# Feature-major input and output in a two-layer float32 encoder trunk

## The chip, the cores and the metric

The kernel runs on one core of a Trainium2 chip. Its time is the device time of one execution in microseconds (us), median of the runs shown. Engines are named as in the profile: PE (TensorE, matmuls and transposes), PEld (its weight loads, which overlap it), DVE (VectorE), ACT (ScalarE), POOL (GpSimd) and SP (SyncE, which here only issues DMAs). PE's clock has two levels, 1.2 and 2.4 GHz; the profile shows the granted one as a share of 2.4 GHz.

## The reference

Two layers (`DEPTH` = 2) work on x of 512 positions by 1024 features, all in float32. Cut to what matters:

```python
for l in range(DEPTH):
    xn = rms_norm(x, norm1_g[l])
    aq, ak, av, bq, bk, bv, cq, ck, cv, cg, gates = split(xn @ w_in[l])
    ya = dilated_mixer(rope(norm(aq)), rope(norm(ak)), av)     # 6 heads, 3 groups
    yb = diff_attention(rope(norm(bq)), rope(norm(bk)), bv)    # 4 heads, two softmax maps each
    yb = rms_norm(yb, b_out_norm_g[l]) * (1.0 - lam_init)      # per head
    yc = silu(cg) * rms_norm(retention(cq, ck, cv), c_out_norm_g[l])   # 4 heads
    g = sigmoid(gates)
    x = x + (g[0]*(ya @ w_br_a[l]) + g[1]*(yb @ w_br_b[l]) + g[2]*(yc @ w_br_c[l])) @ w_o[l]
    x = x + relu(rms_norm(x, norm2_g[l]) @ w_mlp1[l]) ** 2 @ w_mlp2[l]
```

## The kernel before

**Data.** Inside, x lies feature-major: eight tiles of 128 features by 512 positions. Every float32 product is made of three matmuls on rounded halves: a tensor is split into `hi` (a rounded copy, written by ACT) and `lo` (the rest, by DVE), and `gemm` adds hi·hi, hi·lo and lo·hi. In the tile names an `h` or `l` at the end is such a half (`xgh`, `xgl`: x times the norm's gain; `ynh`, `ynl`: a branch's output; `whi`, `wlo`: weights).

**Stages.** The list `sequence` gives the order of the products of a layer: `A` 0 to 2, `cg`, `C` 0 and 1, `B` 0 to 3 (query, key and value columns of one wave each), the gates `G`, the branch outputs `W`, the output product `O`, and then `M1` and `M2`, the two MLP products, in four rounds. Each works in four PSUM banks (`acc`); `pm` holds four more banks for everything else. `G` 1 0 and `G` 1 1 stand right ahead of `W` 1 0 and `W` 1 1, which multiply branch B's four outputs. Weights come in units of two row tiles by SP (`fetch`, four `raw` buffers) and are split a unit ahead (`refine`, two buffers each). `gemm` runs through the units of a product, all four banks for each, and calls `hooks` at the start of a unit and `done` for each bank of the last.

**Order.** Attention runs beside the products as side threads: `thread_prep` (norm and rotation of q and k), `thread_a`, `thread_b` and `thread_c`. In `build` a planner adds up estimated costs per engine and lets a side thread make a step wherever DVE and ACT lie behind PE by its estimate; a thread yields `("need", flag)` until a flag is set, or `("wait", name)` until PE has gone on for `W[name]` us of the estimate. Before, `thread_prep` needs only that a wave's product is done. A scheduler then orders the instructions of each engine, and each engine keeps that order. The rotated q and k of a wave stand in one of two buffers (`qp`, tag `qk`).

**Branch B.** A head ends in `head_norm`: `ps_b_tail` (weighted values, PSUM) is copied to `y` by ACT, turned by four transposes (`ps_yt`), squared and summed by ACT, brought to 1/sqrt by some ten DVE instructions of four columns (`hf` to `hg`), multiplied (`yn`), turned back by four transposes (`ps_yb`) and split into `ynh` and `ynl`.

**Both ends.** x lies position-major in memory. In `main`, 32 transposes (`ps_main`, L823 on) turn the eight input tiles; DVE copies each to `xt`, POOL writes it to `xspill` for the residual of layer 0, and ACT squares the input with a running sum (`sqx`), so that the first norm needs no transposes. `norm_stat` turns the sum into `nr` (1/sqrt per position); the four `acc` banks of A 0 are emptied with `nr` as scale, so A 1 starts after it. In the last layer `M2` is made position-major, for which `thread_xtok` turns x back (32 transposes, `ps_thread_xtok`, each half's eight copies by ACT and DVE), and `done` scales by `r2` per partition and writes 256 KB blocks. In layer 0, `M2` is feature-major and scaled by `rB2`, the statistic spread over partitions by four transposes (`norm_spread`).

The last layer's block as it was:

```python
self.stt(x, b, self.r2[:, o:o + 1], x, OP.mult, OP.add)
eng = self.nc.sync if o % 2 else self.nc.scalar
eng.dma_start(self.outv[:, o, s[2] * 512:(s[2] + 1) * 512], x)
```

Of the kernel before, what the change touches and what calls it, by code (L numbers as in the profile page):

```python
# [65 lines left out]
def weight_plan(sequence):  # L66
    """The weight blocks in the order of use: (array, layer, first row tile, row tiles, columns per row tile)."""
    units, chunks = [], {}
    r = lambda a, n: list(range(a, a + n))
    for l in range(DEPTH):  # L70
        for s in sequence:
# [19 lines left out]
            first = len(units)  # L91
            for k in range(k0, k1, 2):
                units.append((name, l, (k, cols), min(2, k1 - k), sum(c for _, c in cols)))
# [4 lines left out]
def pack_weights(inputs, sequence):  # L98
    """Every weight block laid out as it lands on chip: row in the tile, row tile, column."""
    out = []  # L100
    for (name, l, (k, cols), n, c) in weight_plan(sequence)[0]:
        w = inputs[name][l, k * P:(k + n) * P]
        w = np.concatenate([w[:, a:a + m] for a, m in cols], axis=1)
        out.append(w.reshape(n, P, c).transpose(1, 0, 2).reshape(-1))
    return np.concatenate(out)


class Trunk:
# [44 lines left out]
    def act(self, out, in_, func=AF.Copy, **k):  # L153
        self.cost["ACT"] += 0.19 + self.size(out) / 1000
        self.nc.scalar.activation(out, in_, func, **k)  # L155
# [19 lines left out]
    def stt(self, out, a, s, b, op0, op1):  # L175
        self._d(out, 1.1)
        self.nc.vector.scalar_tensor_tensor(out, a, s, b, op0=op0, op1=op1)  # L177
# [64 lines left out]
    # ---------------------------------------------------------------- weights  # L242
# [58 lines left out]
    # ---------------------------------------------------------------- set-up  # L301
    def setup(self):
# [3 lines left out]
        self.x4 = []  # L306
        rows = self.U((36, P), name="rows")
        nc.scalar.dma_start(rows, a["rows"])
        nc.sync.dma_start(self.blob[:, 0:P], a["blob"][:, 0:P])
        xv = a["x"][0].rearrange("(p j) d -> p j d", j=NJ)  # L310
# [11 lines left out]
        self.fetch(4)  # L322
# [4 lines left out]
        self.identr = cp.tile([P, P], FR, name="identr")  # L327
        self.act(self.identr, self.ident)
        self.gcol = cp.tile([P, 36], FT, name="gcol")
        pt = self.ps(name="ps_setup")  # L330
        self.tr(pt[:, 0:36], rows, self.ident[0:36, 0:36])
        nc.vector.tensor_copy(self.gcol, pt[:, 0:36])
# [5 lines left out]
        self.xspill = [self.dp.tile([KD, P, SEQ], FT, name=f"xspill{l}") for l in range(DEPTH)]  # L338

    def setup2(self):  # L340
        nc, cp, b = self.nc, self.cp, self.blob
        lam = self.tiny(8, "lam", 1)
# [38 lines left out]
    # ---------------------------------------------------------------- norm of x  # L381
# [3 lines left out]
    def norm_feed(self, k, xt):  # L385
# [3 lines left out]
        if "ss" in st:  # L389
            return  # L390
# [32 lines left out]
    # ---------------------------------------------------------------- prep of q, k, v  # L423
# [42 lines left out]
    def prep(self, w, jp):  # L466
# [37 lines left out]
        self.tt(lo, o8, hi_of(s.bitcast(FT)), OP.subtract)  # L504
        yield ("wait", "prep")
# [13 lines left out]
    # ---------------------------------------------------------------- attention pieces  # L519
# [270 lines left out]
    def thread_prep(self, l):  # L790
        first = True
        for s in self.sequence:
# [3 lines left out]
            if first:  # L796
                self.rope_gains(l)
# [11 lines left out]
    # ---------------------------------------------------------------- main stream  # L809
# [7 lines left out]
    def main(self):  # L817
        nc = self.nc
        self.norm_open(0, 0)
        self.refine(AHEAD + 1)  # L820
        self.nrm["ss"] = self.tiny(16, "ss0", 1)
        for k in range(KD):
            b = self.ps(name="ps_main")  # L823
            for j in range(NJ):
                src = self.x4[(k // 2) * 2 + j // 2][:, j % 2, (k % 2) * P:(k % 2 + 1) * P]
                self.tr(b[:, j * P:(j + 1) * P], src, self.ident)
            self.norm_feed(k, b)
            xt = self.U(name="xt")
            self.copy(xt, b, "DVE")
            nc.gpsimd.dma_start(self.xspill[0][k], xt)  # L830
            for i in range(2):
                scr = self.U((P, 256), name="sqx")
                self.act(scr, self.x4[k][:, i, :], AF.Square,
                         accum_out=self.nrm["ss"][:, 4 * (k // 2) + 2 * (k % 2) + i:4 * (k // 2) + 2 * (k % 2) + i + 1])
            yield
        self.x4 = None
        self.setup2()
        for l in range(DEPTH):
            yield from self.layer(l, self.nrm["xg"])

    def layer(self, l, xg):
# [15 lines left out]
        for s in self.sequence:  # L857
            c = self.ch[l, s]
            kind = s[0]
            if kind in ("A", "B", "C"):  # L860
# [4 lines left out]
                w = self.wave_buffers(kind)  # L865
                self.waves[l, kind, s[1]] = w
# [218 lines left out]
```

## Time and profile before

| | us |
|---|---|
| median of 3 runs | 1811.63 (1811.3 to 1813.87) |
| span of the profiled execution | 1812.9 |
| PE busy in it | 1784.7 (98%) |
| DVE, ACT, POOL busy | 1051.4, 795.4, 186.4 |
| granted TensorE clock, mean | 0.994 of full |

The profile is one execution; its span runs from its first to its last instruction. Its own device time is not among the runs shown, so the span stands for it: it lies 0.07% above the median. A row of a timeline gives the start, the length of the instruction (of `xN` of them from the first to the end of the last), engine, line, operation, what is written `<-` what is read, and in brackets how long the engine was idle before it and what ended that. Matmuls overlap, so what one costs is the distance to the next start, not its length.

### The profile page before, as it was taken

The numbers are of one execution on the slowest core, as the hardware profiler recorded it, in microseconds if no ns is written. First come the engines' busy times: TensorE is split into PE (matmuls) and PEld (weight loads), VectorE is DVE, ScalarE is ACT, GpSimd is POOL, SyncE is SP. The second block draws the span as 40 slices with busy tenths as digits, with TensorE's granted clock in tenths as the row PEclk, the third lists the DMA queues.
The fourth block names the chain that finished last, engine by engine and source line by source line (L and its number), as shares of the span: only waits on it lengthen the run. The fifth ranks groups of instructions, "written<-read, shape, count | busy, mean of one in ns | idle before, by whom it ended". The sixth has DMA issues, their size and how long they took to land.

```text
span 1812.9 us, 22187 instructions
## 1 busy us (share of the span) xinstructions
PE 1784.7 (98%) x8433; PEld 1481.1 (82%) x8433; DVE 1051.4 (58%) x1963; ACT 795.4 (44%) x1469; POOL 186.4 (10%) x177
## 2 busy tenths in 40 slices
PE   7999999999999999999999999999999999999999
PEld 6878978877888888888888888788778878888887
DVE  7676787877465333333576767777865552233433
ACT  5555655645334332322345556455543343333241
POOL 1000000011043111111220000000111321111010
PEclk8999999999999999999999999999999999999999
DMA  6221222222233223223332112222212422323222
GB/s 223 88 70 44 85 70 62 79 70 70 82 119 125 93 93 105 93 93 104 105 105 82 65 44 85 71 64 82 80 63 91 141 80 96 102 93 97 101 94 82
DMA packets 49243, 162.78 MB, mean 90 GB/s; under 512 B 5580, under 2 KB 7792, under 8 KB 49008
## 3 DMA queue, kind: packets, MB, share of 16 engines
q1 hardware_dynamic: 45952, 151.91, 25.7%
q0 software_dynamic: 2560, 8.39, 1.4%
q8 instruction: 66, 1.08, 0.3%
q10 hardware_dynamic: 624, 1.07, 0.2%
q14 instruction: 41, 0.34, 0.1%
HBM read 155.05 MB, written 6.29 MB: 89 GB/s over the span
## 4 chain that ended last, share of the span: by engine, by line
PE 93%; DVE 4%; issue 1%; ACT 1%; POOL 0%; DMA 0%; SPq 0%; ACTq 0%; POOLq 0%; DVEq 0%
PE acc L218 81%; PE ps_c_head L218 2%; PE ps_b_scores L218 1%; PE ps_prep L222 1%; PE ps_a_tail L218 1%; PE ps_to_keys L222 1%; PE ps_b_tail L218 1%; PE ps_a_diag_scores L218 1%; PE ps_a_dense_scores L218 1%; DVE wlo L166 1%; DVE xgl L177 1%; DVE part L166 0%; DVE xr L166 0%; PE ps_yt L222 0%; PE ps_yb L222 0%
## 5 line engine op out<-in xcount | busy, mean ns | idle before, releaser
L166 DVE TENSOR_TENSOR wlo<-raw,whi 128x1024 fp32r<-128x1024 f32 (+2 forms) x296 | 351.4, 1187 | 485.9 <-ACT whi L155 484.1
L155 ACT ACTIVATE whi<-raw 128x1024 fp32r<-128x1024 f32 (+2 forms) x296 | 300.0, 1014 | 632.2 <-PE acc L218 558.2
L218 PE MATMUL acc<-xgh,whi 128*128 128x512 f32 x960 | 380.5, 396 | 0.0
L218 PE MATMUL acc<-xgl,whi 128*128 128x512 f32 x960 | 375.7, 391 | 0.0
L218 PE MATMUL acc<-xgh,wlo 128*128 128x512 f32 x960 | 374.8, 390 | 0.0
L218 PEld LDWEIGHTS acc<-xgh,whi 128*128 128x128 f32 x960 | 180.6, 188 | 39.5 <-issue 3.1
L218 PEld LDWEIGHTS acc<-xgh,wlo 128*128 128x128 f32 x960 | 180.6, 188 | 38.3
L218 PE MATMUL acc<-whi,xgh 128*128 128x384 f32 (+1 forms) x576 | 208.7, 363 | 1.5 <-DVE vl L177 0.8
L218 PEld LDWEIGHTS acc<-xgl,whi 128*128 128x128 f32 x960 | 180.8, 188 | 35.4
L218 PE MATMUL acc<-wlo,xgh 128*128 128x384 f32 (+1 forms) x576 | 202.8, 352 | 2.0 <-DVE wlo L166 2.0
L218 PE MATMUL acc<-whi,xgl 128*128 128x384 f32 (+1 forms) x576 | 201.0, 352 | 0.1
L163 POOL TENSOR_TENSOR gate<-gate,gate 128x512 f32<-128x512 f32 x32 | 50.4, 1590 | 926.5 <-DVE gate L177 562.8
L163 POOL TENSOR_TENSOR rl<-rl 128x512 f32<-128x512 f32 x64 | 78.5, 1236 | 537.4 <-ACT hh L155 429.7
L218 PEld LDWEIGHTS acc<-whi,xgh 128*128 128x128 f32 x576 | 109.6, 191 | 13.2 <-issue 5.4
L218 PEld LDWEIGHTS acc<-wlo,xgh 128*128 128x128 f32 x576 | 109.9, 191 | 7.6 <-DVE wlo L166 2.3
L218 PEld LDWEIGHTS acc<-whi,xgl 128*128 128x128 f32 x576 | 109.5, 190 | 6.5 <-issue 0.7
L218 PE MATMUL acc<-hh,wlo 128*128 128x512 f32 x256 | 99.7, 389 | 0.9 <-DVE wlo L166 0.9
L218 PE MATMUL acc<-hl,whi 128*128 128x512 f32 x256 | 99.6, 389 | 0.0
L218 PE MATMUL acc<-hh,whi 128*128 128x512 f32 x256 | 99.6, 389 | 0.0
L218 PE MATMUL acc<-whi,hh 128*128 128x512 f32 x256 | 99.6, 389 | 0.0
L218 PE MATMUL acc<-wlo,hh 128*128 128x512 f32 x256 | 99.6, 389 | 0.0
L218 PE MATMUL acc<-whi,hl 128*128 128x512 f32 x256 | 99.6, 389 | 0.0
(218 smaller groups left out, 2741.8 us busy)
## 6 DMA issues: line engine op xcount, KB each, us to landing
raw<-in_weights_dram SPq DMA_DIRECT2D x236, 512.0 KB, 3.3
raw<-in_weights_dram SPq DMA_DIRECT2D x56, 384.0 KB, 3.1
xr<-xspill POOLq DMA_DIRECT2D x16, 256.0 KB, 4.1
x<-in_x_dram SPq DMA_DIRECT2D x8, 256.0 KB, 5.8
xspill<-xt POOLq DMA_DIRECT2D x8, 256.0 KB, 3.5
xspill<-xr POOLq DMA_DIRECT2D x8, 256.0 KB, 2.3
blob<-in_blob_dram SPq DMA_DIRECT2D x1, 1024.0 KB
raw<-in_weights_dram SPq DMA_DIRECT2D x4, 256.0 KB, 2.6
```

What stands on the lines that cost most here:

```text
L155: self.nc.scalar.activation(out, in_, func, **k)
L163: self.nc.gpsimd.tensor_tensor(out, a, b, op=op)
L166: self.nc.vector.tensor_tensor(out, a, b, op=op)
L177: self.nc.vector.scalar_tensor_tensor(out, a, s, b, op0=op0, op1=op1)
L218: self.nc.tensor.matmul(out, lhsT, rhs, start=start, stop=stop)
L222: self.nc.tensor.transpose(out, in_, ident)
```

## The change

x enters as an array of eight feature-major tiles and is loaded straight into the tiles `xt`, in turn with the first weight units, of which the first two have one row tile instead of two; identity and gains come over ACT's queue, the gains already turned (`cols` for `rows`). The transposes, the copies and the writes to `xspill` at the start are gone; layer 0's residual reads the input. The first norm is made as the others are: `norm_square` (ACT squares a tile, POOL adds it to the sum), then four transposes of the sum (`ps_norm`). `first_hooks` spreads the splits and squares over the units of A 0. `setup2` and `rope_gains` come after the last split of x (`fed`). `thread_prep` of wave i now needs wave i-2 to be done before its rotated q and k are written (`w["free"]`). The last layer's `M2` is feature-major as layer 0's is, with `rB2`, and the output is written feature-major, in halves of 256 columns. In both layers the partial sum is scaled and added to x already in the third of the four rounds.

```diff
-            for k in range(k0, k1, 2):
-                units.append((name, l, (k, cols), min(2, k1 - k), sum(c for _, c in cols)))
+            first, k = len(units), k0
+            while k < k1:
+                n = min(1 if not units or len(units) == 1 else 2, k1 - k)
...
-        for q in range(4):
-            for jp in range(2):
-                t = self.U((P, 2, 256), name="x4")
-                nc.sync.dma_start(t, xv[:, 2 * jp:2 * jp + 2, q * 256:(q + 1) * 256])
-                self.x4.append(t)
-            self.fetch((1, 1, 2, 2)[q])
-        self.fetch(3)
+        for k in range(KD):
+            t = self.U(name="xt")
+            nc.sync.dma_start(t, a["x"][k])
+            self.xin.append(t)
+            self.fetch((1, 2, 2, 3, 3, 4, 4, 5)[k])
...
-        self.xspill = [self.dp.tile([KD, P, SEQ], FT, name=f"xspill{l}") for l in range(DEPTH)]
+        self.xspill = [a["x"], self.dp.tile([KD, P, SEQ], FT, name="xspill")]
...
-        if st["sq"] is None:
-            self.rsum(m, st["ss"].rearrange("p (q j) -> p j q", q=4))
-        else:
-            b = self.ps(name="ps_norm")
-            for j in range(NJ):
-                self.tr(b[:, j * P:(j + 1) * P], st["sq"][:, j * P:(j + 1) * P], self.ident)
-            self.rsum(m, b.rearrange("p (j f) -> p j f", j=NJ))
+        b = self.ps(name="ps_norm")
+        for j in range(NJ):
+            self.tr(b[:, j * P:(j + 1) * P], st["sq"][:, j * P:(j + 1) * P], self.ident)
+        self.rsum(m, b.rearrange("p (j f) -> p j f", j=NJ))
...
+        yield ("need", w["free"])
         yield ("wait", "prep")
...
-                self.rope_gains(l)
+                with self.tc.issue_after(self.fed[0]), self.tc.issue_after(self.fed[1]):
+                    if l == 0:
+                        self.setup2()
+                    self.rope_gains(l)
...
-        for k in range(KD):
-            b = self.ps(name="ps_main")
-            for j in range(NJ):
-                src = self.x4[(k // 2) * 2 + j // 2][:, j % 2, (k % 2) * P:(k % 2 + 1) * P]
-                self.tr(b[:, j * P:(j + 1) * P], src, self.ident)
-            self.norm_feed(k, b)
-            xt = self.U(name="xt")
-            self.copy(xt, b, "DVE")
-            nc.gpsimd.dma_start(self.xspill[0][k], xt)
...
+        for k in range(2):
+            self.refine(k + 1)
+            self.norm_feed(k, self.xin[k], False)
...
+        return [feed((2, 3), ()), feed((4, 5), (0, 1)), feed((6, 7), (2, 3)), feed((), (4, 5, 6, 7)), stat]
...
+                w["free"] = ("done", l) + waves[i - 2] if i >= 2 else ("start",)
...
-                        self.rB2 = None if last else self.norm_spread(self.r2)
+                        self.rB2 = self.norm_spread(self.r2)
...
+                    elif s[1] < 3:
+                        self.tt(part[k], part[k], b, OP.add)
+                        if s[1] == 2:
                             t = part.pop(k)
-                            self.tt(t, t, b, OP.add)
                             self.tt(t, t, self.rB2, OP.mult)
-                            x = self.xt[k]
                             self.tt(x, x, t, OP.add)
...
+                        for cs in ((slice(0, 256), slice(256, 512)) if last else (slice(0, 512),)):
+                            self.tt(t[:, cs], b[:, cs], self.rB2[:, cs], OP.mult)
+                            self.tt(x[:, cs], x[:, cs], t[:, cs], OP.add)
+                            if last:
+                                eng = self.nc.sync if o % 2 else self.nc.scalar
+                                eng.dma_start(self.outv[k][:, cs], x[:, cs])
...
-    def thread_xtok(self):
```

What that does to the order of the engines is shown at three places. The numbers behind the names count tiles.

PE, before, at the end of A 0 (`acc` 291 to 294) and the start of A 1 (`acc` 461 on); `ps_norm` here is `norm_spread`:

```order
L218 MATMUL acc_294<-whi_351,xgh_255 128x384
L218 MATMUL acc_294<-wlo_352,xgh_255 128x384
L218 MATMUL acc_294<-whi_351,xgl_256 128x384
L222 MATMUL ps_norm_521<-blob,nr_87_384 128x128 x4
L218 MATMUL acc_461<-whi_400,xgh_143 128x384
L218 MATMUL acc_461<-wlo_401,xgh_143 128x384
```

PE, of the changed kernel, inside A 0 (`acc` 149 to 152), where the last of its five units begins; `sq` is the sum of squares that POOL adds up:

```order
L220 MATMUL acc_152<-whi_218,xgh_177 128x384
L220 MATMUL acc_152<-wlo_219,xgh_177 128x384
L220 MATMUL acc_152<-whi_218,xgl_178 128x384
L224 MATMUL ps_norm_291<-blob,sq_181 128x128 x4
L220 MATMUL acc_149<-whi_260,xgh_204 128x384
L220 MATMUL acc_149<-wlo_261,xgh_204 128x384
```

The transposes of the sum of squares, which the kernel before has not got here, stand ahead of the last 24 matmuls of A 0.

PE, before, ahead of `W` 1 0 of layer 0: branch B's last head is turned (`ps_yt`) inside `G` 1 1 (`acc` 4729 to 4732):

```order
L218 MATMUL acc_4729<-xgh_159,wlo_4639 128x512
L218 MATMUL acc_4730<-xgh_143,whi_4638 128x512
L222 MATMUL ps_yt_4697<-blob,y_4695 128x128 x4
L218 MATMUL acc_4730<-xgl_144,whi_4638 128x512
L218 MATMUL acc_4730<-xgh_143,wlo_4639 128x512
L218 MATMUL acc_4730<-xgh_159,whi_4638 128x512
L218 MATMUL acc_4730<-xgl_160,whi_4638 128x512
```

PE, of the changed kernel, inside `W` 1 0 of layer 0 (`acc` 4806 to 4809), the last rows of branch B's last head (`ps_b_tail`, `ps_yt`, `ps_yb`):

```order
L220 MATMUL ps_b_tail_4714<-wTh_4756,vl_3222 128x512
L220 MATMUL acc_4808<-ynl_4711,whi_4810 128x512
L220 MATMUL acc_4808<-ynh_4710,wlo_4811 128x512
L220 MATMUL acc_4809<-ynh_4710,whi_4810 128x512
L220 MATMUL acc_4809<-ynl_4711,whi_4810 128x512
L224 MATMUL ps_yt_4765<-blob,y_4763 128x128 x4
L220 MATMUL acc_4809<-ynh_4710,wlo_4811 128x512
L224 MATMUL ps_yb_4797<-blob,yn_4795 128x128 x4
L220 MATMUL acc_4806<-ynh_4802,whi_4810 128x512
L220 MATMUL acc_4807<-ynh_4802,whi_4810 128x512
```

Before, 35 `acc` matmuls stand between `ps_yt` and `ps_yb` of that head and 54 more of `G` 1 1 behind `ps_yb`; now one stands between them, and the next row reads its output. The third head moved likewise: its `ps_yt` stands behind the 11th matmul of `W` 1 0, and 13 matmuls stand between that and its `ps_yb`. Layer 1 has the same rows.

POOL, of the changed kernel, at the program's start (before, eight writes of `xt` to `xspill` stand there, the memsets among and behind them):

```order
L165 TENSOR_TENSOR sq_181<-sq_181,sq_183 128x512
L165 TENSOR_TENSOR sq_181<-sq_181,sq_212 128x512
L165 TENSOR_TENSOR sq_181<-sq_181,sq_215 128x512
L165 TENSOR_TENSOR sq_181<-sq_181,sq_248 128x512
L165 TENSOR_TENSOR sq_181<-sq_181,sq_251 128x512
L165 TENSOR_TENSOR sq_181<-sq_181,sq_254 128x512
L165 TENSOR_TENSOR sq_181<-sq_181,sq_257 128x512
L431 MEMSET vh_367 128x4x64
```

Seven adds in a chain now feed `ps_norm`. On ACT the squares of the tiles 2 to 7 stand behind `edec`, which reads `small`, the 14th of SP's loads.

## Rows read from the trace of the kernel before

**Rows 1.** The page: shares of the chain of work that ended last

```profile
PE 93%; DVE 4%; issue 1%; ACT 1%; POOL 0%; DMA 0%; SPq 0%; ACTq 0%; POOLq 0%; DVEq 0%
```

**Rows 2.** What PE waited for: total us, times, longest us

```profile
PE ps_norm L222 <- DVE nr L177: 6.0, 1, 6.0
...
PE ps_b_tail L218 <- DVE wTl L166: 3.1, 3, 1.2
...
PE acc L218 <- DVE wlo L166: 2.9, 2, 2.0
...
PE ps_thread_xtok L222 <- DVE xtok L214: 2.6, 1, 2.6
...
PE ps_norm L222 <- POOL sq L163: 1.5, 2, 1.3
```

**Rows 3.** Busy time by stretch; the first line names the columns

```profile
core 0: us, PE busy (x) PEld busy (x) DVE busy (x) ACT busy (x) POOL busy (x), PEclk, DMA share, GB/s
...
40.00:45.00 5.00, 5.00 (x20) 5.00 (x20) 4.12 (x17) 2.29 (x7) 0.00 (x0) 0.60 0.00 0
```

**Rows 4.** Timeline of the start; columns as explained under the table

```profile
9.86 0.67 PE L218 MATMUL acc<-whi,xgh 128*128 128x384 f32 x1
...
15.18 0.22 ACT L155 ACTIVATE edec<-small 128x16 f32<-128x16 f32 x1 [0.16 <-DMA small<-in_small_dram]
...
31.89 2.72 DVE L173 TENSOR_SCALAR nm<-nm 128x4 f32<-128x4 f32 x1
...
39.54 0.66 PE L218 MATMUL acc<-whi,xgh 128*128 128x384 f32 x1 [0.77 <-DVE vl L177]
```

**Rows 5.** DMA issues: engine, count, KB each, us to landing (median)

```profile
small<-in_small_dram SPq DMA_DIRECT2D x1, 520.0 KB, 7.0
...
out_dram<-xtok SPq DMA_DIRECT2D x4, 256.0 KB, 2.0
```

**Rows 6.** Groups of instructions: count, busy us, mean ns, idle before

```profile
L177 DVE SCALAR_TENSOR_TENSOR xgl<-xr,gcol,xgh 128x512 fp32r<-128x512 f32 x24 | 26.1, 1088 | 0.3
...
L177 DVE SCALAR_TENSOR_TENSOR xgl<-ps_main,gcol,xgh 128x512 fp32r<-128x512 f32 x8 | 6.0, 745 | 0.4 <-ACT xgh L155 0.4
...
L166 DVE TENSOR_TENSOR o<-t,blob 128x256 f32<-128x256 f32 x16 | 6.2, 417 | 0.0
```

**Rows 7.** POOL's adds of squares: ns min/median/max, first and last start us

```profile
L163 POOL TENSOR_TENSOR sq<-sq,sq x21: 1290/1482/2164, 539.2 to 1455.9; 128x512 f32<-128x512 f32 x21
```

**Rows 8.** Timeline of one head of branch B in layer 0

```profile
472.75 0.39 PE L218 MATMUL ps_b_tail<-wTh,vl 128*128 128x512 f32 x1
...
474.56 0.60 PE L222 MATMUL ps_yt<-blob,y 128*128 128x128 f32 x4
...
478.81 0.69 DVE L166 TENSOR_TENSOR yn<-ps_yt,hg 128x512 f32<-128x512 f32 x1
...
482.97 0.60 PE L222 MATMUL ps_yb<-blob,yn 128*128 128x128 f32 x4
...
483.61 0.69 ACT L155 ACTIVATE ynh<-ps_yb,ghead 128x512 fp32r<-128x512 f32 x1 [3.69 <-PE ps_yb L222]
...
484.41 0.75 DVE L177 SCALAR_TENSOR_TENSOR ynl<-ps_yb,ghead,ynh 128x512 fp32r<-128x512 f32 x1 [3.23 <-ACT ynh L155]
```

**Rows 9.** PE: first rows of M1 0 and M2 0 by layer, and xtok

```profile
560.98 0.39 PE L218 MATMUL acc<-xgh,whi 128*128 128x512 f32 x1
...
605.96 0.39 PE L218 MATMUL acc<-hh,whi 128*128 128x512 f32 x1
...
1452.21 0.39 PE L218 MATMUL acc<-xgh,whi 128*128 128x512 f32 x1
...
1459.18 1.56 PE L222 MATMUL ps_thread_xtok<-blob,xr 128*128 128x128 f32 x12 [2.56 <-DVE xtok L214]
...
1504.16 0.39 PE L218 MATMUL acc<-whi,hh 128*128 128x512 f32 x1
```

**Rows 10.** Timeline: the last instruction of DVE

```profile
1809.00 0.75 DVE L177 SCALAR_TENSOR_TENSOR xtok<-acc,nr,xtok 128x512 f32<-128x512 f32 x1 [0.61 <-PE acc L218]
```

More of the change, by code (lines that the diff above doesn't have):

```diff
@@ L90, in weight_plan @@
                 name, cols, k0, k1 = "w_mlp2", [(s[2] * 512, 512)], s[1] * 8, s[1] * 8 + 8
-            first = len(units)
-            for k in range(k0, k1, 2):
-                units.append((name, l, (k, cols), min(2, k1 - k), sum(c for _, c in cols)))
+            first, k = len(units), k0
+            while k < k1:
+                n = min(1 if not units or len(units) == 1 else 2, k1 - k)
+                units.append((name, l, (k, cols), n, sum(c for _, c in cols)))
+                k += n
             chunks[l, s] = (first, len(units))
@@ L383, in norm_open, with norm_feed @@
         self.nrm = {"col": which * 16 + l * 8, "xg": [None] * KD, "sq": None}
-    def norm_feed(self, k, xt):
+    def norm_feed(self, k, xt, square=True):
         st = self.nrm
@@ L388, in norm_feed, with norm_square @@
         st["xg"][k] = self.split(xt, "xg", scale=g)
-        if "ss" in st:
-            return
+        if square:
+            self.norm_square(xt)
+    def norm_square(self, xt):
+        st = self.nrm
         sq = self.U(name="sq")
@@ L925, in layer @@
                     x2 = self.nrm["xg"]
-                    if last:
-                        self.side.append([self.thread_xtok(), None])
             elif kind == "M1":
@@ new lines, in layer, with done @@
+                if s[1] == 3 and s[2] == 0 and not last:
+                    self.norm_open(0, l + 1)
+                def done(o, b):
+                    k = s[2] * 4 + o
+                    x = self.xt[k]
+                    if s[1] == 0:
+                        t = self.U(name="part")
+                        self.act(t, b)
+                        part[k] = t
+                    elif s[1] < 3:
+                        self.tt(part[k], part[k], b, OP.add)
+                        if s[1] == 2:
@@ L980, in done @@
                             t = part.pop(k)
-                            self.tt(t, t, b, OP.add)
                             self.tt(t, t, self.rB2, OP.mult)
-                            x = self.xt[k]
                             self.tt(x, x, t, OP.add)
-                            self.xt[k] = None
+                    else:
+                        t = self.U(name="fin")
+                        self.xt[k] = None
+                        for cs in ((slice(0, 256), slice(256, 512)) if last else (slice(0, 512),)):
[4 more added lines that the diff above has]
+                                eng.dma_start(self.outv[k][:, cs], x[:, cs])
+                        if not last:
@@ L986, in done @@
                             self.nc.gpsimd.dma_start(self.xspill[l + 1][k], x)
                             self.norm_feed(k, x)
-                yield from self.gemm(c, h, done, last)
-    def thread_xtok(self):
-        self.xtok = [self.U(name="xtok") for _ in range(8)]
-        for j in range(NJ):
-            for hf in range(2):
-                b = self.ps(name="ps_thread_xtok")
-                for k in range(4):
-                    self.tr(b[:, k * P:(k + 1) * P], self.xt[hf * 4 + k][:, j * P:(j + 1) * P], self.ident)
-                self.copy(self.xtok[hf * 4 + j], b, "DVE" if hf else "ACT")
-                yield
-        self.xt = None
-        self.flags.add(("xtok",))
+                yield from self.gemm(c, h, done, False)
@@ L1025, in build @@
         self.waves, self.y, self.silu, self.side = {}, {}, {}, []
-        self.outv = self.a["out"][0].rearrange("(p j) d -> p j d", j=NJ)
+        self.flags.add(("start",))
+        self.outv = self.a["out"]
         self.plan()
@@ L1083 @@
     r = run_bass_kernel_spmd(nc, [arrays], core_ids=[0])
-    return r.results[0]["out_0_dram"]
+    out = np.asarray(r.results[0]["out_0_dram"]).reshape(KD, P, NJ, P)
+    return np.ascontiguousarray(out.transpose(3, 2, 0, 1).reshape(1, SEQ, D))
```

82 lines of the change are left out of this document (23 added, 59 removed).

## The prediction

> **What bounds the kernel now.** I read the chain of waits first: PE carries 93% of it [rows 1], so the kernel lasts as long as PE works, plus the places where PE stands still. Those are in the list of what PE waited for [rows 2]: 6.0 us at the start for the first norm's `nr`, 2.6 us for a copy of `thread_xtok`, 2.9 us for `wlo` (two waits) and 1.5 us for POOL's sums of squares (two waits), the last two kinds mostly where layer 0 ends and layer 1 begins, and 3.1 us in three steps of branch B's tails. Nothing else waits as long, so the change can gain only there and by PE work that it removes, and it loses wherever it makes PE wait anew. A wait costs more than itself: after the one at the start the stretch from 40 to 45 us was granted 0.60 of the clock, a mix of the two levels [rows 3], which is 2.0 us lost in five. The start is a chain from x to A 1: the first `acc` matmul at 9.86 us, `nm` at 31.89, A 1 at 39.54 [rows 4].
>
> **The start: -7.5 us.** The 32 transposes and eight copies go, and x no longer passes through PSUM. That would bring A 0 forward by several us, but the statistic now hangs on a longer chain, and A 1 waits for it. In the order the squares of tiles 2 to 7 stand on ACT behind `edec`, which waits for `small`. Before, `edec` ran at 15.18, right as `small` landed 7.0 us after its issue [rows 4, 5]. By the code some 3.2 MB stand ahead of it on SP before and 3.5 MB now, so I take 15.9. One square (0.6) and six adds on POOL follow in a chain. An add took 1.29 to 2.16 us, median 1.48 [rows 7]: 8.9 us (7.7 to 13). The sum is there at 25.6 (24.4 to 29.7). Its four transposes stand in PE's row ahead of A 0's last 24 matmuls, so PE, done with the first four units before, waits for POOL here; that wait is new. From `nm` to A 1 it took 39.54 - 31.89 = 7.65 us [rows 4], in which `nm`, an instruction on four columns, lasted 2.72 us; without that stall I put the stretch at 5.1. The changed order adds the sum over the transposed squares (a pass over 128x512 in PSUM, 0.7 by [rows 6]) and two instructions on the decay table `T` (896 and 128 columns; 0.9, an estimate), hence 6.7 from `ps_norm`. A 1 then starts at 25.6 + 0.5 + 6.7 = 32.8. The memsets among which `nm` stalled follow POOL's last add directly, so the stall can return (0 to 2.5); I take 0.7, and A 1 at 33.5, 6 us sooner. Because A 0's last unit now runs behind `ps_norm`, PE idles less right before A 1, and of the 2.0 us at the lower clock I take 1.5 as gained. Bounds: 31.6 and the whole clock loss give -10; 39.4 gives 0.
>
> **The end of layer 1's attention: -7.0 us.** `thread_xtok` is measured by the distance between the first matmuls of M1 0 and M2 0: 44.98 us in layer 0, 51.95 in layer 1 [rows 9], 6.97 more. Layer 0 has four transposes of `norm_spread` in this stretch that layer 1 has not; the change brings them there, so the two stretches become equal and the whole 6.97 goes (6.5 to 7.2). The same rows give the price of a stop: 32 transposes at 0.108 (twelve in 1.56 us with the last one's length) are 3.46 us, the wait 2.56; 6.97 + 0.43 - 3.46 - 2.56 leaves 1.4 us lost behind a stop of 2.56.
>
> **The seam between the layers: -3 us.** The last round of layer 0's M2 has one DVE instruction less per tile, and the one that goes reads two operands from SBUF. Waits of up to 4.4 us lie in its reach [rows 2]; that all go is unlikely, since `xgl` and `wlo` still queue there. I take -3 (-1 to -4.4). The two instructions per tile that move into the third round run beside 43 us of matmuls; if that cover failed they would cost up to 1 us: +0.3 (0 to 1).
>
> **The last tile: +0.6 us.** Before, one DVE instruction of 0.75 us [rows 10] and a DMA of 2.0 [rows 5] end the program. Now four of 128x256 stand there, in the order two products, then two sums; one such takes 0.417 [rows 6] or less where they overlap, 1.35 to 1.67 in all, +0.6 to +0.9; the last DMA is half as large and saves 0 to 0.7 of the 2.0. I take +0.6 (-0.1 to +1.2).
>
> **Branch B's last heads: +22 us.** This is the term that decides. `need w["free"]` puts the writing of q and k behind the end of the wave before last, in the planner's order. The side work of each layer comes later, and the end of branch B has moved from `G` 1 1 into `W` 1 0, as the order shows. There PE has nothing else to do: `W` 1 1 needs the same four banks. What a head takes is in [rows 8]. From the last `ps_b_tail` to `ps_yt` 474.56 - 472.75 = 1.8 us (eight matmuls, 0.226 each). From `ps_yt` to the end of `yn` 478.81 + 0.69 - 474.56 = 4.9, with the hand-over 5.0. From `ps_yb` to the end of `ynh` 483.61 + 0.69 - 482.97 = 1.33, to the end of `ynl` 484.41 + 0.75 - 482.97 = 2.2. Before, the whole distance was filled: PE reached `ps_yb` at 482.97, 3.5 us after `yn`. Now, for the fourth head, PE has five matmuls for the 1.8 (0.67 idle), four transposes and one matmul, 0.66 us, for the 5.0 (4.3 idle), four transposes for the 1.33 (0.9) and two matmuls more for the 2.2 (0.4): 6.3 us. For the third head four transposes and 13 matmuls, 3.4 us, stand against the 5.0 (1.6), and eight transposes against the 1.33 (0.5): 2.1. Between the two heads four steps of `ps_b_tail` follow each other with little beside them; three such waits lasted 3.1 us before [rows 2], and I add one of their mean, 1.0. That is 9.4 us per layer. The clock falls after such stops; 1.4 us behind 2.56 idle and 2.0 or more behind 6.0 [rows 3, 9] let me take 1.7. Two layers: 2 x 11.1 = 22. Bounds: the four gaps that hardly depend on DVE and ACT being busy (0.67, 4.3, 0.9, 1.6) alone, at full clock, 2 x 7.5 = 15; two falls of the clock per layer, 2 x 13.4 = 27.
>
> The other moves lie under PE's work: the smaller first weight units, gains over ACT's queue, `setup2` later on DVE (its instructions queue behind `xgl`, ahead of `nm`, and are in the 6.7), layer 0's residual from the input.
>
> **Sum.** -7.5 - 7.0 - 3.0 + 0.3 + 0.6 + 22 = +5.4. Against the profiled span of 1812.9 that is 1818.3; the median lies 1.3 lower, and 1811.63 + 5.4 = **1817.0**.
>
> **Rivals.** First, *the bare gaps*, which ends on the other side: the heads cost 15, because the clock stays at its upper level through gaps that are broken up by short work, and the start gains its full 10 with POOL's adds at 1.29. Then 1811.63 - 10 - 7 - 4.4 + 0.9 + 15 = 1806, faster. For it: no stop except the 4.3 is as long as those that were followed by the lower clock; against it, a stop of 2.56 was enough at `xtok`. It decides from a cost of about 9 us per layer down and an A 1 before 32 us.
>
> Second, *POOL and DVE in each other's way at the start*. `xgl` took 745 ns where its input came from PSUM and 1088 where it came from SBUF, beside POOL's adds, and these took between 1.29 and 2.16 [rows 6, 7]; now both halves of it stand at the start, the adds as well as six splits that read SBUF. With adds of 2.16 and `nm` stalled again A 1 starts at 39.4, as before: the start gains nothing, and the sum is 1811.63 - 7.0 - 3.0 + 0.9 + 22 = 1824.5. It decides from adds of 2 us up. The Trainium skill has a rule on this ("GPSIMD Engine Reference", section "Specifications"): POOL shares its SBUF interfaces with VectorE and contends with instructions that read two SBUF inputs. It speaks against moving the statistic to POOL here; the two means above agree with it. By the rule the time would be the 1824.5, by the median add the 1817.
>
> Third, *the heads are hidden after all*: the tails' work is done early enough that PE finds each row ready, and the rest of the sum stays. Then 1811.63 - 16.6 = 1795. For it speaks that before nothing of branch B's ends stopped PE; against it the order, in which PE's row behind `ps_yt` is all but followed by `ps_yb`, while `yn` lies 4.9 us of small DVE and ACT steps away. The order would have to mean less than it says.
>
> **How the numbers follow.** Forecast 0.52, bare gaps 0.20, contention 0.20, hidden heads 0.08. A measurement of this kernel tells some 0.2% (3.6 us) from no change: faster is under 1808.0, slower over 1815.25. Faster: the hidden heads and half of the bare gaps, with the low tail of the forecast, 0.20. Slower: contention and 0.30 of the forecast, 0.50. Same: the rest, 0.30. The forecast's own range is 1809 to 1825. The range for all has to leave out the hidden heads and a little on both sides: 1805 to 1827.
>
> **What would show it.** The start: `ps_norm` in A 0 waiting for POOL's `sq`, at about 21 to 26 us, and A 1 at 33.5; if A 1 comes before 32 or after 37, a rival has it. The heads: in each layer a stretch in `W` 1 0 with PE waiting for `yn` some 4 us and 9 us in all, followed by matmuls at the lower clock; if the waits there add up to less than 6 us per layer, this step is wrong. M1 0 to M2 0 should be 45 us in both layers, the wait for `wlo` at the seam under 1 us. The forecast is wrong as a whole if side work delayed elsewhere (the waves of `C`, the heads of `A`) stops PE as well, or if the gaps in `W` 1 0 are filled.

## The result: 1840.0 us, 1.5% slower

The changed kernel took 1840.03 us (median of four runs, 1838.49 to 1842.54), the kernel before 1811.47; the ratio is 1.0153 with a 95% interval of 1.0139 to 1.0168. The forecast was 1817.0 within 1805 to 1827: the side was right, the size was not. The span of the profiled execution went from 1812.9 to 1837.4, 24.5 us more. Runs of the kernel before lie at two levels, near 1811 and 1815, and the one profiled is of the upper; so medians give 28.6 us and the two traces 24.5. A span is no device time: a run of the kernel before lasts some 1.9 us longer than its span, which puts the profiled one at 1814.8, 3.3 us above the median; the profiled run of the changed kernel (1840.47) lasts 3.1 us longer than its span. Stages are compared by the traces.

The chain that ended last, from the page of the changed kernel (answers [rows 1]), and what PE waited for (answers [rows 2]; total us, times, longest us):

```profile
PE 89%; DVE 7%; ACT 2%; issue 1%; POOL 1%; DMA 0%; DVEq 0%; ACTq 0%; POOLq 0%
```

```profile
PE ps_yb L224 <- DVE yn L168: 12.0, 6, 4.3
...
PE ps_b_tail L220 <- ACT wTh L157: 4.5, 4, 2.0
PE ps_norm L224 <- POOL sq L165: 4.5, 4, 3.3
PE acc L220 <- DVE vl L179: 4.4, 2, 3.6
PE acc L220 <- ACT ynh L157: 2.2, 4, 0.8
PE acc L220 <- DVE wlo L168: 1.0, 1, 1.0
```

PE's share of the chain fell from 93% to 89%. The wait of 6.0 for `nr`, the 2.6 for `thread_xtok` and the 2.9 for `wlo` at the seam are gone; new are 12.0 for `yn`, 3.6 of the 4.4 for `vl`, 2.2 for `ynh`, 3.3 in one wait for POOL's `sq`, 1.0 for `wlo` in A 0 of layer 0, and `ps_b_tail` waits for `wTh` where it waited for `wTl`.

Where the 24.5 us lie is read from the first matmul of each product, before and after:

| stretch | before | after | difference |
|---|---|---|---|
| start to A 2 of layer 0 | 58.34 | 53.16 | -5.2 |
| A 2 to O 0, layer 0 | 459.1 | 479.7 | +20.6 |
| O 0 of layer 0 to A 2 of layer 1 | 433.2 | 431.1 | -2.1 |
| A 2 to O 0, layer 1 | 458.0 | 475.7 | +17.7 |
| O 0 to M1 1, layer 1 | 73.7 | 66.7 | -7.0 |
| M1 1 of layer 1 to the end | 330.5 | 331.0 | +0.5 |

The stretches A 2 to O 0, in which the attention runs beside the products, lost 38.3 us; all other stretches gained 13.8. The largest piece is `W` 1 0, here in layer 0 (timeline, PE, with the third and the fourth head of branch B; answers [rows 8]):

```profile
499.94 0.39 PE L220 MATMUL acc<-ynh,wlo 128*128 128x512 f32 x1
501.74 0.66 PE L224 MATMUL ps_yb<-blob,yn 128*128 128x128 f32 x4 [1.41 <-DVE yn L168]
...
503.17 0.96 PE L220 MATMUL acc<-ynh,whi 128*128 128x512 f32 x3 [0.34 <-ACT ynh L157]
...
510.42 0.60 PE L224 MATMUL ps_yt<-blob,y 128*128 128x128 f32 x4
510.78 0.48 PE L220 MATMUL acc<-ynh,wlo 128*128 128x512 f32 x1
515.50 1.09 PE L224 MATMUL ps_yb<-blob,yn 128*128 128x128 f32 x4 [4.25 <-DVE yn L168]
517.37 1.22 PE L220 MATMUL acc<-ynh,whi 128*128 128x512 f32 x2 [0.78 <-ACT ynh L157]
518.39 0.63 PE L220 MATMUL acc<-ynl,whi 128*128 128x512 f32 x1
518.82 0.63 PE L220 MATMUL acc<-ynh,wlo 128*128 128x512 f32 x1
```

PE stands still for 1.41 us ahead of the third head's `ps_yb` and for 4.25 ahead of the fourth's, then 0.78 for `ynh`. The matmuls behind it start 0.43 us apart instead of 0.23: the granted clock of that stretch was 0.50, the lower level (by stretch; the first line names the columns):

```profile
core 0: us, PE busy (x) PEld busy (x) DVE busy (x) ACT busy (x) POOL busy (x), PEclk, DMA share, GB/s
...
510.00:515.00 5.00, 1.25 (x8) 0.75 (x6) 2.33 (x14) 1.43 (x9) 0.00 (x0) 0.92 0.01 2
515.00:520.00 5.00, 3.72 (x10) 2.77 (x11) 1.63 (x3) 0.69 (x1) 0.00 (x0) 0.50 0.00 0
```

`W` 1 0 took 27.75 us in layer 0 and 28.08 in layer 1. Its 48 matmuls and twelve of `ps_b_tail` at 0.227 and 32 transposes at 0.108 are 17.1 us of work, so 10.7 and 11.0 were lost there: PE's waits are 6.8 us in each layer, and most of the rest is the lower clock. That leaves 16.6 us lost in other places of the two stretches. The longest are the first matmul of `G` 2 0, which waits for B 3's values to leave the bank, and a `ps_b_tail` of the second head (timeline, PE, layer 0; layer 1 has the second alike):

```profile
342.75 0.47 PE L220 MATMUL acc<-xgh,whi 128*128 128x512 f32 x1 [3.58 <-DVE vl L179]
...
438.46 0.50 PE L220 MATMUL ps_b_tail<-wTh,vh 128*128 128x512 f32 x1 [1.90 <-ACT wTh L157]
```

Behind these three stops the granted clock was 0.50 from 344 to 347 us, 0.52 from 439 to 442 and 0.50 from 1344 to 1350 (layer 1). PE's waits outside `W` 1 0 add up to 11.0 us and the lower clock costs some 6 more (an estimate from these stretches); the kernel before lost some 7 us in waits and at the lower clock here. So some 10 of the 16.6 us are placed; the rest stands in no listed wait, and its cause stays open.

### The profile page after: what moved, and what is told of

Read it like the earlier page. It is cut to its first block, busy times and chain, and to the rows that moved or that the text cites. A ratio compares the mean times of both kernels' runs of the same rounds, so it can differ in the third digit from the quotient of the medians.

```text
span 1837.4 us, 22093 instructions
## 1 busy us (share of the span) xinstructions
PE 1792.4 (98%) x8376; PEld 1475.1 (80%) x8376; DVE 1063.5 (58%) x1991; ACT 793.7 (43%) x1443; POOL 190.8 (10%) x176
## 4 chain that ended last, share of the span: by engine, by line
PE 89%; DVE 7%; ACT 2%; issue 1%; POOL 1%; DMA 0%; DVEq 0%; ACTq 0%; POOLq 0%
PE acc L220 77%; PE ps_c_head L220 2%; PE ps_b_scores L220 1%; DVE wlo L168 1%; PE ps_b_tail L220 1%; PE ps_prep L224 1%; PE ps_a_tail L220 1%; PE ps_to_keys L224 1%; PE ps_a_diag_scores L220 1%; DVE rt L168 1%; PE ps_a_dense_scores L220 1%; ACT y L157 0%; ACT whi L157 0%; PE ps_yb L224 0%; POOL sq L165 0%
## 5 line engine op out<-in xcount | busy, mean ns | idle before, releaser
L220 PE MATMUL acc<-hh,whi 128*128 128x512 f32 x512 | 199.3, 389 | 0.3 <-DVE fin L168 0.3
L220 PE MATMUL acc<-hh,wlo 128*128 128x512 f32 x512 | 199.2, 389 | 0.0
L220 PE MATMUL acc<-hl,whi 128*128 128x512 f32 x512 | 199.2, 389 | 0.0
L220 PEld LDWEIGHTS acc<-hh,whi 128*128 128x128 f32 x512 | 96.1, 188 | 21.0 <-DVE fin L168 1.0
L220 PEld LDWEIGHTS acc<-hl,whi 128*128 128x128 f32 x512 | 96.1, 188 | 19.9
L220 PEld LDWEIGHTS acc<-hh,wlo 128*128 128x128 f32 x512 | 96.1, 188 | 19.8
```

The costliest lines, as they stand in the source:

```text
L220: self.nc.tensor.matmul(out, lhsT, rhs, start=start, stop=stop)
```

## The experiments

Eleven kernels besides a repetition were run, timed in alternation with the kernel before, whose median lay between 1811.5 and 1814.4 in the sessions; ratios are to the kernel before of the same session. One table holds what they have in common: whether the need is there, the planner's number `SLACK` (a side thread steps while DVE and ACT lie behind PE plus `SLACK` by the estimate: at -3 they must lie more than 3 us behind, above 0 they may be ahead), where the last head's `ps_yb` stands, counted in `acc` matmuls of its layer (`W` 1 0 begins at 1704), and what the stretch from A 2 to O 0 took over the kernel before in its trace.

| kernel | need | SLACK | last ps_yb, layers 0, 1 | A 2 to O 0, us over before | median |
|---|---|---|---|---|---|
| before | no | -3 | 1650, 1650 | 0, 0 | 1811.5 |
| mlp_alone | no | -3 | 1650, 1650 | +0.1, +1.3 | 1804.5 |
| need_alone | yes | -3 | 1740, 1740 | +22.1, +14.2 | 1850.9 |
| changed | yes | -3 | 1740, 1740 | +20.6, +17.7 | 1840.0 |
| adds_on_dve | yes | -3 | 1740, 1740 | +22.3, +16.2 | 1836.8 |
| dve_adds_slack_m2p5 | yes | -2.5 | 1740, 1733 | +9.8, +5.7 | 1816.8 |
| slack_m2 | yes | -2 | 1704, 1704 | +1.8, +3.0 | 1804.8 |
| dve_adds_slack_m2 | yes | -2 | 1704, 1704 | 0.0, +3.0 | 1801.7 |
| dve_adds_slack_m1 | yes | -1 | 1686, 1680 | +4.3, +6.5 | 1807.1 |
| slack_0 | yes | 0 | 1674, 1674 | +5.0, +4.9 | 1810.7 |
| dve_adds_slack_1p5 | yes | 1.5 | 1662, 1560 | +5.6, +6.9 | 1810.5 |
| dve_adds_slack_3 | yes | 3 | 1620, 1554 | +8.8, +1.8 | 1810.1 |
| mlp_slack_0 | no | 0 | 1542, 1530 | +12.4, +11.9 | 1832.3 |

Two traces of the kernel before differ by +1.7 and -1.4 us in these two stretches, so a difference of under some 2 us tells nothing.

**The need alone.** The kernel before with

```diff
+        yield ("need", w["free"])
         yield ("wait", "prep")
...
+                w["free"] = ("done", l) + waves[i - 2] if i >= 2 else ("start",)
...
```

> The kernel before with only the added need in thread_prep (the writing of q and k of a wave waits for the end of the wave before last). Its order in W 1 0 is that of the changed kernel in both layers. Theory 1, the need costs all that the two attention stretches lost (in the two traces 20.6 and 17.7 us from A 2 to O 0): 1811.5 + 36 to 39 = 1849. Rival, the need costs only the uncovered heads in W 1 0, as forecast, and the rest comes with the other start: 1811.5 + 20 to 23 = 1833.

It took 1850.9 us, 1.0206 of before (1.0191 to 1.0221). Its trace has the old start and `thread_xtok`, and the waits of the changed kernel's attention:

```profile
PE ps_yb L222 <- DVE yn L166: 11.9, 6, 4.2
PE ps_norm L222 <- DVE nr L177: 6.0, 1, 6.0
PE ps_b_tail L218 <- ACT wTh L155: 4.6, 4, 2.0
PE acc L218 <- DVE vl L177: 4.3, 2, 3.6
```

The waits for `yn`, `wTh` and `vl` are those of the changed kernel to 0.1 us, and the two stretches lost 36.3 us against 38.3 (3.5 less in layer 1, where the waits are the same 10.5 us but the granted clock was higher, 0.993 against 0.986). Theory 1 holds: the need alone brings the whole loss in the attention, also the part outside `W` 1 0; that it does so by where it puts the side work, the runs with other `SLACK` show below. The rival, which was the forecast's step, falls.

**The last product alone.** The kernel before with the feature-major M2 and output:

```diff
-                        self.side.append([self.thread_xtok(), None])
...
+                        self.rB2 = self.norm_spread(self.r2)
...
-                if last:
-                    def done(o, b):
-                        key = (s[2], o)
...
+                                eng.dma_start(self.outv[k][:, cs], x[:, cs])
...
```

> The kernel before with only the last layer's M2 and the output feature-major (no thread_xtok, scaling in round three, last blocks in halves). By the traces: -7.0 for thread_xtok, about -2 at the seam, +0.5 at the end: 1803. If the 2 to 3 us by which the changed kernel's timed runs exceed its spans (before: about 0) come from writing the output in halves, they show here too and the time is 1805 to 1806.

1804.5 us, 0.9952 of before (0.9937 to 0.9967). By the trace -7.0 from O 0 to M1 1, -2.2 at the seam, +0.5 at the end, as expected. This half of the change is a gain by itself. Its runs last 1.8 to 1.9 us longer than their spans, as those of the kernel before do (my "about 0" set a profiled span against the median of other runs), so writing the output in halves costs nothing beyond the span. Of the 4 us between traces and medians 3.3 are the level of the profiled run of the kernel before, and about 1 the 3.1 us of the changed kernel's profiled run, whose cause stays open.

**The planner's number.** The changed kernel with

```diff
-SLACK = -3.0
+SLACK = 0
```

> The changed kernel with one number of the planner changed, SLACK from -3 to 0 us, so that side threads may step earlier; the need stays. In its order the last heads' ps_yt stands at acc matmul 1636 and ps_yb at 1674 of a layer, 68 and 30 matmuls ahead of W 1 0's first row at 1704, instead of inside W 1 0. Theory 1 (late side work is the loss, whatever makes it late): 1840 - 33 to -40 = 1800 to 1807, below the kernel before. Rival (the need itself stops prep and so the engines, wherever the rows stand): 1825 to 1840.

1810.7 us: 29 us of the loss come back with the need still there. That is 4 us above the range that I expected: A 2 to O 0 still took 9.9 us more than before. So the need does not stop the engines by itself; the place of the rows does (the runs with -2 below, in which the need stands too, lose 3.0 and 4.9 us). Two steps further in the same direction, with the adds on DVE (below):

```diff
-SLACK = -3.0
+SLACK = 1.5
```

> The changed kernel with the adds of squares on DVE and SLACK at 1.5. In its order the last heads' ps_yb stands at acc matmul 1662 of layer 0 and 1560 of layer 1, both ahead of W 1 0 at 1704. Theory 1 (late side work is the loss): all of the 29 us that SLACK 0 gave back stays back, and the start gives the 3 to 4 us of the adds on DVE: 1803 to 1807, below the kernel before. Rival (earlier side work only moves the waits to other places): 1810 or more.

> As the run with 1.5, SLACK at 3: ps_yb of the last head at acc matmul 1620 and 1554. Theory 1 with all rows covered: the gain has levelled off, within 2 us of the run with 1.5. Rival (side work that is too early makes PE wait for DVE and ACT): 4 us or more above it.

1810.5 and 1810.1. The first expectation was missed, and the rival's 1810 came: all heads end ahead of `W` 1 0, and 12.5 and 10.6 us are lost elsewhere. The second was met in its number, though not all rows are covered. Side work can stand too early as well. The control shows it without the need:

> The kernel before with only the feature-major M2 and output, as in the run of it alone (1804.5), and SLACK at 0; no need. Its last ps_yb moves from acc matmul 1650 to 1542 of layer 0. A control: theory 1 says that SLACK gives nothing where the heads already end ahead of W 1 0, 1802 to 1807. Rival, SLACK 0 is faster by itself and the 29 us were partly that: below 1800.

1832.3 us, 28 more than `mlp_alone`, from `SLACK` alone. Its last heads are covered by far, and PE waits here instead, 14.6 us in the two attention stretches against 3.5 in `mlp_alone` (what PE waited for):

```profile
PE ps_yb L222 <- DVE yn L166: 4.3, 2, 3.2
PE acc L218 <- DVE vl L177: 4.1, 4, 2.8
...
PE acc L218 <- DVE gate L177: 2.3, 2, 2.0
```

The rival "SLACK 0 is faster by itself" falls, and my expectation of no difference with it: where everything is covered, moving side work ahead makes new collisions, now with `yn` of other heads and with banks that DVE has not emptied. Then two steps between:

> The changed kernel with the adds of squares on DVE and SLACK at -1. The runs so far say that side work can stand too late (need with -3: 36 us more from A 1 to O 0 of both layers than before) and too early (no need with 0: 26 us more), and 0 with the need still cost 8.6. In the order of this one the last ps_yb stands at acc matmul 1686 and 1680, 18 to 24 ahead of W 1 0. If cover behind ps_yb is what counts it is as good as 0 or better: 1803 to 1808. If each SLACK only shifts which rows collide: 1810 to 1815.

> As the run with -1, SLACK at -2: the last ps_yb stands at acc matmul 1704, right ahead of W 1 0, and what needs its output comes 40 matmuls later (ynh of the fourth head is read in the second unit). Theory: heads just covered, no wait for yn over 1 us in W 1 0; other waits between those of 0 and -3: 1808 to 1818. Rival (a steep edge, the clock falls as in the changed kernel): 1825 or more.

1807.1, in the range for cover behind `ps_yb`, and 1801.7, below its range and 0.9933 of before (0.9916 to 0.9949): the fastest kernel here. With that number alone, POOL's adds as in the changed kernel:

```diff
-SLACK = -3.0
+SLACK = -2
```

> The changed kernel with SLACK at -2 and nothing else. Theory 1 (the planner's number that puts the side work, not the change's parts, cost the 29 us): as the run with adds on DVE and -2 (1801.7) plus the 3 to 4 us of POOL's adds at the start: 1804 to 1807. Rival (the adds on DVE had a share in the better order): 1812 or more.

1804.8 us, 0.9954 of before (0.9938 to 0.9971), as expected. All of the change's parts are in it, and it beats both kernels. It does not beat `mlp_alone` (1804.5, 0.9952): most of the 5.8 us that its start gains goes into the 4.9 that the attention still loses. Only with the adds on DVE is the whole change ahead of that half of it, by 2.8 us in the medians, with intervals of the ratios that overlap. Whether -2 helps a kernel without the need was not tried. Its waits:

```profile
PE ps_norm L224 <- POOL sq L165: 3.8, 4, 2.6
PE acc L220 <- DVE wlo L168: 1.6, 1, 1.6
PE ps_yb L224 <- DVE yn L168: 1.1, 2, 0.8
```

What remains is the start (`sq`, `wlo`); the wait for `yn` is 1.1 us in two pieces where the changed kernel has 12.0 in six. The last step asks how steep the edge is:

> Adds on DVE, SLACK at -2.5: a step between. In its order only the fourth head lies inside W 1 0: 13 matmuls between its ps_yt and ps_yb in layer 0, 18 in layer 1, against 1 in the changed kernel and a covered head at -2. By the head's price (5.0 us from ps_yt to ps_yb against 0.43 + 0.227 per matmul) PE waits 1.6 us in layer 0 and 0.5 in layer 1, and some 1 to 2 us more for ynh and ynl: 1801.7 + 3 to 6 = 1805 to 1808. Rival (the heads' cover is not what counts): the same 1802 as at -2, or as far off as the changed kernel.

1816.8 us, outside what I expected. The head's price held roughly: 2.1 us ahead of the last `ps_yb` in layer 0 where 1.6 was worked out, and 0.4 in layer 1 where it was 0.5. Part of the rest is again in other rows, which I had not looked at in its order (what PE waited for):

```profile
PE ps_b_tail L220 <- DVE wTl L168: 4.8, 5, 2.2
PE ps_yb L224 <- DVE yn L168: 3.5, 4, 2.1
```

**The adds on DVE.** The changed kernel with

```diff
-    def norm_square(self, xt):
+    def norm_square(self, xt, eng="POOL"):
...
-            self.tt(st["sq"], st["sq"], sq, OP.add, eng="POOL")
+            self.tt(st["sq"], st["sq"], sq, OP.add, eng=eng)
...
-                    self.norm_square(self.xin[k])
+                    self.norm_square(self.xin[k], "DVE")
```

> The changed kernel with the seven adds of squares of the first norm on DVE instead of POOL; all else as changed. In the changed kernel's trace the small rope instructions on DVE lasted 1.25 to 1.84 us beside POOL's adds, 0.18 without, and ps_norm waited 3.3 us for POOL. Theory (the two engines are in each other's way, and the POOL chain sets A 1): A 1 starts at 30 to 32 instead of 36.4 and the time is 1840 - 4 to -6 = 1835. Rival (DVE's own queue of rope gains ahead of the statistic sets it): A 1 at 35 or later, 1838 to 1840.

1836.8 us. A 1 starts at 30.74 (timeline, PE):

```profile
21.96 0.66 PE L224 MATMUL ps_norm<-blob,sq 128*128 128x128 f32 x4
...
28.79 0.65 PE L224 MATMUL ps_norm<-blob,nr 128*128 128x128 f32 x4 [2.00 <-DVE nr L179]
30.74 0.41 PE L220 MATMUL acc<-whi,xgh 128*128 128x384 f32 x1 [1.30 <-DVE vl L179]
```

`ps_norm` no longer waits for POOL and A 1 comes 5.6 us sooner; 4 us of it are left at A 2 and 3.2 in the medians. DVE's products of 32 columns all took 0.18 us here and the copies 0.28. The first theory holds, with A 1 in its range and the time 0.8 us above it.

**The kernel before once more.**

> The kernel before once more, for its profile. Its runs lie at two levels, 1811 and 1815; the profile shown (span 1812.9) is of the upper. If this one is of the lower (span 1809), the place of the 4 us shows by comparing the two traces stage by stage: at the start, if it is how x lands or how long PE runs at its lower clock there; spread over the weight units, if it is the memory.

1813.7 us with a span of 1811.9: the upper level again, so at which places the 4 us lie stays open. What they go with, the recorded clocks tell: of 52 runs of the kernel before, the 22 from 1810.7 to 1812.5 us had a mean granted clock of 0.996 or 0.997, the 30 from 1812.8 to 1815.7 one of 0.994 or 0.995, and 0.002 to 0.003 of 1811 us is 3.6 to 5.4 (an estimate from these). The two traces of the same program differ by steps of 1.4 to 1.7 us, up and down. One lies behind `thread_xtok`, where PE stopped 2.56 us in the one trace and 2.57 in the other (by stretch, the earlier trace and this one):

```profile
1460.00:1466.00 6.00, 6.00 (x27) 4.87 (x25) 1.26 (x2) 0.99 (x2) 0.00 (x0) 0.72 0.00 0
```

```profile
1460.00:1466.00 6.00, 6.00 (x36) 5.17 (x35) 2.50 (x5) 1.66 (x2) 0.00 (x0) 1.00 0.01 4
```

After the same stop the clock was at its lower level for part of the one execution, and never below the upper in the other; that is 1.6 us. Another such step, the other way, lies between 160 and 170 us, where the granted clock was 1.00 and 0.83. Nor does every fall stand behind a stop: from 150 to 160 us of the first trace PE was busy all the time, no wait of it is listed near, and the clock was at its lower level for part of it:

```profile
150.00:160.00 10.00, 10.00 (x45) 8.23 (x45) 6.46 (x10) 5.39 (x14) 0.00 (x0) 0.84 0.08 16
```

Not tried: the changed start without the need. What the need is for, no run shows.

## Why the prediction was wrong

**The step that failed** is the one on the need: it priced the side work's new place only in `W` 1 0 and took the rest as covered. `W` 1 0 itself had the right mechanism: 22 us forecast, 21.7 measured, with 4.3 us ahead of the fourth head's `ps_yb` (4.25), 1.6 for the third (1.41), then the lower clock. That the sum fits so well is in part luck: the waits were 6.8 us per layer instead of 9.4 (none ahead of the fourth `ps_yt`, none between the heads), while the clock was granted 0.52 from 514 to 521 us and 0.51 from 1422 to 1429, which cost some 3.4 per layer instead of 1.7. But the same shift also moved the waves' ends and the second head's tail, and other places than `W` 1 0 cost 16.6 us more: among them 3.6 us for B 3's `vl` in layer 0 and 1.9 and 2.0 for the second head's `wTh`, with the lower clock behind each. `need_alone` loses as much, so the need brings it; some 6 us of it are placed at no row. The last sentence of the prediction named this as what would make it wrong ("if side work delayed elsewhere ... stops PE as well") and gave it no chance and no price; the places that it names (the waves of `C`, the heads of `A`) are not the ones that cost most. I had read the order at one place, where the shift was plain, and not at the other places that the same shift reached.

**The start**: -7.5 forecast, -5.2 measured at A 2 (the old start took 57.25 to 58.93 us in five traces, so 1 us of difference tells little here). The chain was right up to `ps_norm` (rows of ACT, POOL, PE of the changed kernel; answer [rows 4]):

```profile
16.96 0.20 ACT L157 ACTIVATE edec<-small 128x16 f32<-128x16 f32 x1
```

```profile
14.98 1.30 POOL L165 TENSOR_TENSOR sq<-sq,sq 128x512 f32<-128x512 f32 x1 [13.18 <-ACT sq L157]
17.84 8.81 POOL L165 TENSOR_TENSOR sq<-sq,sq 128x512 f32<-128x512 f32 x6 [1.56 <-ACT sq L157]
```

```profile
8.91 0.69 PE L220 MATMUL acc<-whi,xgh 128*128 128x384 f32 x1 [8.91 <-ACT xgh L157]
...
23.04 0.34 PE L220 MATMUL acc<-whi,xgl 128*128 128x384 f32 x1
26.70 1.11 PE L224 MATMUL ps_norm<-blob,sq 128*128 128x128 f32 x4 [3.32 <-POOL sq L165]
...
29.13 0.69 PE L220 MATMUL acc<-wlo,xgh 128*128 128x384 f32 x1 [0.99 <-DVE wlo L168]
...
36.38 0.44 PE L220 MATMUL acc<-whi,xgh 128*128 128x384 f32 x1 [0.80 <-DVE vl L179]
```

`edec` ran at 16.96 (15.9 forecast), six adds took 8.8 us (8.9), `ps_norm` started at 26.70 (25.6). From there to A 1 it took 9.7 us instead of 7.9. The mis-sized term is DVE's queue ahead of `nm`: the second rival had the mechanism, but laid it on the adds, which at 1.47 us each were as before. It was DVE's small instructions that took longer beside POOL's adds:

```profile
21.17 1.28 DVE L168 TENSOR_TENSOR Sg<-gs,blob 128x32 f32<-128x32 f32 x1
...
22.58 1.37 DVE L168 TENSOR_TENSOR Cg<-small,blob 128x32 f32<-128x32 f32 x2
...
25.45 1.84 DVE L216 COPY Cg<-gs 128x256 f32<-128x256 f32 x1
...
27.31 0.18 DVE L168 TENSOR_TENSOR Sg<-gs,blob 128x32 f32<-128x32 f32 x1
...
28.13 0.94 DVE L168 TENSOR_TENSOR wlo<-raw,whi 128x768 fp32r<-128x768 f32 x1
...
30.06 0.68 DVE L191 TENSOR_REDUCE nm<-ps_norm 128x4 f32<-128x512 f32 x1
...
31.52 0.15 DVE L175 TENSOR_SCALAR nm<-nm 128x4 f32<-128x4 f32 x1
```

Products of 32 columns took 1.28 and 1.27 us (the first of the two in the row of 1.37) and a copy 1.84 while POOL added, and the products 0.18 when it had ended; with the adds on DVE they took 0.18 and the copies 0.28, so POOL's adds are the cause. So the split of the last weights ran at 28.13 and the sum over squares at 30.06, over 2 us after its input. `nm` itself took 0.15; the stall that I allowed 0.7 for did not return, since DVE reached it when the memsets were over. A 1 now runs at the upper clock, which gave 2.0 us (1.5 forecast): the lower level came earlier, from 27 to 33 us (granted 0.50), when A 1 still waited for `nr`. x in its new layout gained only 1 us at the first matmul (8.91): ACT splits the second weight unit, landed at 7.7, before it splits x.

**thread_xtok**: -7.0 forecast, -7.0 measured. Of it 5.4 us are work and stop (5.6 in the forecast); the other 1.6 are the luck of one trace, since in the second trace of the kernel before no lower clock followed the stop, and the distance is 50.33 instead of 51.95. Now M1 0 to M2 0 is 44.96 and 44.98 us in the two layers (first rows of M1 0 and M2 0; answer [rows 9]):

```profile
576.36 0.39 PE L220 MATMUL acc<-xgh,whi 128*128 128x512 f32 x1
...
621.32 0.39 PE L220 MATMUL acc<-hh,whi 128*128 128x512 f32 x1
...
1483.17 0.39 PE L220 MATMUL acc<-xgh,whi 128*128 128x512 f32 x1
...
1528.15 0.39 PE L220 MATMUL acc<-hh,whi 128*128 128x512 f32 x1
```

**The seam**: -3 forecast, -2.1 measured; the waits for `wlo` there (2.9) are gone, as foreseen, and POOL's `sq` (0.7) and `fin` (0.5) still stop PE. **The last tile**: +0.6 forecast, +0.5 measured, with two products and two sums of 256 columns at the end of DVE (answer [rows 10]):

```profile
1832.99 0.76 DVE L168 TENSOR_TENSOR fin<-acc,rB 128x256 f32<-128x256 f32 x2
1833.66 0.75 DVE L168 TENSOR_TENSOR xr<-xr,fin 128x256 f32<-128x256 f32 x2
```

**The base.** The forecast took the profiled span for a device time that lies 1.3 us above the median; with the 1.9 us between span and run it lies 3.3 above. So the terms were read from a trace of the upper level and added to a median of the lower; 3 to 4 us of the miss by medians are that and the changed kernel's longer distance between span and run. Of the 19 us by traces, 16.6 are the other places, 2.3 the start.

Of the rivals, the bare gaps (A 1 came at 36.4, and the clock fell in `W` 1 0) and the hidden heads fall with the rows above. Contention was given 0.20 and a time of 1824.5; its mechanism was there, and took some 2 us of the start's gain instead of all 7.5.

## To carry to other kernels

Where engines keep the order that a planner wrote, a new dependence in the planner is a change of the whole order: read from the two orders what each of its consumers stands next to, everywhere, before any of its parts is priced. Retune the planner's number after such an edit: here -2 for -3 was worth 35 us, and the number is not smooth (with the adds on DVE 1816.8 at -2.5, 1801.7 at -2, 1807.1 at -1). A chain of serial small steps, here 5 us of normalisation, needs its own length of independent matmuls behind it in PE's row, or PE waits for what is not covered; here it waited 4.25 us and then ran at its lower clock. And measure the parts of a change alone: here half of it (1804.5) was worth as much as the whole with the number retuned (1804.8).

## What was not expected of the hardware

Beside each of POOL's last six adds one short DVE instruction lasted until the add had ended: products of 32 columns 1.25 to 1.28 us against 0.18, `edec` (8 columns) 1.26 against 0.16, copies of 256 columns 1.39 and 1.84 against 0.28; others beside the same adds ran at 0.18. The adds that began at 19.58, 21.07, 22.48 and 23.88 us ended at 21.00, 22.40, 23.80 and 25.18, the long DVE instructions beside them at 21.15, 22.45, 23.85 and 25.23. The copy of 1.84 outlasted the last add by 0.6 us, into the memsets. I had looked for the effect on wide instructions. The Trainium skill ("GPSIMD Engine Reference", section "Specifications") says that POOL shares its SBUF interfaces with VectorE and names instructions with two SBUF inputs; the products of 32 columns agree. The copies and `edec` have one input from SBUF, and no row tells whether they ran in the two-port mode that the page names beside.

A stop of PE does not always cost the clock: the same stop of 2.6 us was followed by 1.4 to 1.6 us of loss in one execution and by none in the next. The 1.7 us per layer of the forecast were therefore one of several outcomes; in the changed kernel's trace the lower clock came, and cost twice that. The two levels of the kernel before, 4 us apart, go with the mean granted clock; whether they are a sum of such outcomes, no run shows, since both traces are of the upper.
